# Attention weights copied into float32r tiles before they are transposed, in a one-core hybrid attention layer

## The chip, the core and the metric

The kernel runs on one NeuronCore of a Trainium2 chip. Its instructions go to five in-order queues: TensorE (PE; its weight loads are listed apart as PEld), VectorE (DVE), ScalarE (ACT), GpSimd (POOL) and SyncE (SP, which here only issues DMAs). The metric is the device time of one execution in microseconds, as the median of several runs. Operands are 4-byte floats. [...] 

## The reference

One residual layer over x (1024 x 1024). A conditioning vector gives a shift, a scale and a gate. The normalised input u is multiplied by a wide projection into queries, keys, values and gates of 16 heads of width 64. Eight heads are stick-breaking attention, eight are forgetting attention, both causal. The gated head outputs go through an output projection, and a residual and a layer norm end it:

```python
u = layer_norm(x) * (1 + scale) + shift
h = u @ w_in                        # q, k, v, g of 8 forgetting heads and of 8 stick-breaking heads
s = q @ k.T * 64 ** -0.5            # per head and block of 128 queries, keys up to the block's end
p = softmax(s + f_q - f_k)          # forgetting heads, masked causally
w = exp(log_sigmoid(s) + later)     # stick-breaking heads, later = sum of log_sigmoid(-s) of later keys
y = concat(p @ v, w @ v) * silu(g)
x = layer_norm(alpha * x + gate * (y @ w_out), ln_g, ln_b)
```

## The kernel before

**Units.** Heads go in eight pairs: 0 to 3 stick-breaking, 4 to 7 forgetting. A unit (p, h, i) is one head h of pair p and one block i of 128 queries against (i+1) x 128 keys, so there are 128 units, 16 per pair. A unit makes its scores on TensorE in PSUM (L483, L484), turns them into weights `be` or `a`, an SBUF tile of 128 queries by up to 1024 keys (ACT L506, L508, DVE scans L514, L518 and POOL L520, L521 for the stick-breaking pairs; DVE L491, ACT L496, POOL L499 for the others), and transposes them block by block on TensorE (L537), since the product with the values wants the keys on the partitions. Up to four transposes fill one PSUM tile `T`, of which there are two. ACT copies it out rounded (L539, hi) and DVE subtracts (L540, lo). The product with the values (`pv`, L554) runs for two query blocks at a time.

**Order on TensorE.** The order of TensorE is written out by hand. In turn k the scores of unit k are issued, and the transposes of unit k - LAG (LAG is 2), with `weights_turn`; `att_transpose` also puts waiting `pv` products behind its first T tile. Between them go "fillers", a generator of the projections of later pairs: `gen_m(p, m)` makes queries (m = 0), keys (1) or gates (2) of pair p in two PSUM accumulators, with 24 matmuls of 512 columns each, and `gen_v(g)` the values of two pairs in eight accumulators, with 24 matmuls of 256 columns each. The accumulators `acc` have two buffers. `FILL` says how many filler steps go into each pair's units. The other engines' orders come from a planner; a wait there holds up all that stands behind it on that engine.

**Tiles.** Queries and keys of a pair are four tiles of 128 x 1024 (one per head), from a ring `q` of four buffers and a ring `k` of four, so two pairs fit. `evac_k` fills half of a key tile by a DMA inside SBUF (L298). `xr`, the input block of the output stage, uses the same ring at the end.

Of the kernel before, what the change touches and what calls it, by code (L numbers as in the profile page):

```python
# [7 lines left out]

F32 = mybir.dt.float32
# [4 lines left out]
P = 128  # L14
# [3 lines left out]
NPAIR = 8  # L18
# [9 lines left out]
def tile_hybrid_layer(  # L28
# [30 lines left out]
    def pt_tile(name, dt=F32R, shape=None):  # L59
        return big("pt", 3, name, dt, shape or [P, 2, 1024])  # L60

    def acc_tile(name):
        return ps.tile([P, 512], F32, tag="acc", bufs=2, name=name)

# [23 lines left out]
        return stack  # L88


    ident = cp.tile([P, P], F32, tag="ident", name="ident")
    make_identity(nc, ident)
    causal = cp.tile([P, P], F32, tag="causal", name="causal")
    nc.gpsimd.memset(causal, 0.0)
    nc.gpsimd.affine_select(out=causal, in_=causal, pattern=[[-1, P]], base=0,
# [221 lines left out]
    key_casts = []  # L317

    def make_q(p):
        qst[p] = [big("q", 4, f"q_{p}_{h}", F32R) for h in range(2)]  # L320

    def make_k(p):
        kst[p] = [big("k", 4, f"k_{p}_{h}", F32R) for h in range(2)]
        klo[p] = big("kl", 2, f"kl_{p}", F32R)

    def make_g(p):
# [124 lines left out]
    def att_query(u):  # L451
# [3 lines left out]
        r = slice(h * HD, h * HD + HD)  # L455
        nc.scalar.copy(z[r, :], qst[p][h].bitcast(F32)[r, i * P:i * P + P])  # L456

    masks, scaled, lows, gates = [], [], [], []

    def att_causal(u):  # L460
# [9 lines left out]
    def att_scores(u, following):  # L470
        p, h, i = u
        z = zq.pop(u)
        ke = (i + 1) * P
        ns = 1 if ke <= 512 else 2
        w = ke // ns
        qs = slice(i * P, i * P + P)
        if p >= 4:
            f = fb[2 * (p - 4) + h]
        S = s_tile(f"S_{p}_{h}_{i}")
        halves = range(ns) if p >= 4 else range(ns)[::-1]  # L480
        for s in halves:
            ks = slice(s * w, s * w + w)
            nc.tensor.matmul(S[:, s, :w], qst[p][h][:, qs], kst[p][h][:, ks], start=True, stop=False)  # L483
            nc.tensor.matmul(S[:, s, :w], z, klo[p][:, ks], start=False, stop=True)  # L484
        v3 = lambda a: a[:, :ke].rearrange("p (a b) -> p a b", a=ns)
        if p >= 4:
            a = att_tile(f"a_{p}_{h}_{i}")
            nm = sb.tile([P, 1], F32, tag="nm", bufs=4, name=f"nm_{p}_{h}_{i}")
            l = sb.tile([P, 1], F32, tag="l", bufs=4, name=f"l_{p}_{h}_{i}")
            with after(*lows):  # L490
                nc.vector.tensor_tensor_reduce(out=v3(a), in0=S[:, :ns, :w], in1=v3(f),  # L491
                                               op0=ALU.add, op1=ALU.min, scale=-1.0, scalar=BIG,
                                               accum_out=nm)
            if following:
                att_causal(following)
            nc.scalar.activation(a[:, :ke], a[:, :ke], AF.Exp, scale=-1.0, bias=nm, accum_out=l)  # L496
            nc.vector.reciprocal(l, l)  # L497
            scaled[:] = [*scaled[-3:],
                         nc.gpsimd.tensor_scalar(a[:, :ke], a[:, :ke], l, 1.0, op0=ALU.mult, op1=ALU.mult)]  # L499
            st_w[u] = a  # L500
        else:
            kp = att_tile(f"kp_{p}_{h}_{i}")
            be = att_tile(f"be_{p}_{h}_{i}")
            with after(*key_casts):
                for s in halves:
                    nc.scalar.activation(kp[:, s * w:s * w + w], S[:, s, :w], AF.Sigmoid, scale=-1.0)  # L506
            key_casts.clear()
            last_act = nc.scalar.activation(v3(be), S[:, :ns, :w], AF.Sigmoid)  # L508
            gates[:] = [last_act]


            lo = ke - w
            rv = kp[:, lo:ke][:, ::-1]
            last_dve = nc.vector.tensor_tensor_scan(rv, rv, floor[:, :ke - lo], initial=0.0,  # L514
                                                    op0=ALU.mult, op1=ALU.max)
            if lo:
                rv = kp[:, :lo][:, ::-1]
                last_dve = nc.vector.tensor_tensor_scan(rv, rv, floor[:, P:P + 1].to_broadcast([P, lo]),  # L518
                                                        initial=kp[:, lo:lo + 1], op0=ALU.mult, op1=ALU.max)
            nc.gpsimd.tensor_tensor(be[:, :ke - 1], be[:, :ke - 1], kp[:, 1:ke], op=ALU.mult)  # L520
            nc.gpsimd.memset(be[:, ke - 1:ke], 0.0)  # L521
            st_w[u] = be
            return last_act, last_dve

    def att_transpose(u, between=()):
        p, h, i = u
        a = st_w.pop(u)
        j, qo = i // 2, (i % 2) * P
        for g in range((i // 4) + 1):
            n = min(4, i + 1 - 4 * g)  # L530
            if (p, h, j, g) not in st_pt:
                st_pt[p, h, j, g] = pt_tile(f"pt_{p}_{h}_{j}_{g}", F32R, [P, 2, 4, 256])
            hi, lo = (st_pt[p, h, j, g][:, x] for x in range(2))
            tp = t_tile(f"T_{p}_{h}_{i}_{g}")
            for b in range(n):
                kb = 4 * g + b
                nc.tensor.transpose(tp[:, b * P:(b + 1) * P], a[:, kb * P:(kb + 1) * P], ident)  # L537
            t3 = tp[:, :n * P].rearrange("p (a b) -> p a b", a=n)
            nc.scalar.copy(hi[:, :n, qo:qo + P], t3)  # L539
            lows[:] = [nc.vector.tensor_tensor(lo[:, :n, qo:qo + P], t3, hi.bitcast(F32)[:, :n, qo:qo + P],  # L540
                                               op=ALU.subtract)]
            while between:
                att_pv(*between.pop(0))
# [56 lines left out]

    def start_raw(n):
        if used[0] % 2 == 0:
            raws.append(big("qk"[len(raws) // 4], 4, f"raws_{len(raws)}"))
        a = used[0] % 2 * 512
        used[0] += n
        return raws[-1][:, a:a + n * 512]
# [336 lines left out]
    def o_half(t, h):  # L943
# [1 line left out]
        s = slice(*groups(t)[h])  # L945
        ng = len(groups(t))
        if h == 0:
            xr = big("k", 4, f"xr_{t}")
# [67 lines left out]
    def gen_last_g(p):  # L1016
# [26 lines left out]
    LEAD = 2  # L1043
    LAG = 2
    W0 = 100.0
    OUT0 = 4
    TAIL = (2, 2, 2, 2, 2, 2, 4, 4, 4, 4, 8)
# [35 lines left out]
    tail = chain([gen_out_first(6), gen_out_last(6)] + [gen_out(t) for t in OUT_ORDER[1:]])  # L1083
    fill(4)
    def weights_turn(k):
        if LAG <= k < len(units) + LAG:
            u = units[k - LAG]
            att_transpose(u, ready)
            seen.add(u)
            if (u[0], u[1], u[2] ^ 1) in seen:  # L1090
                ready.append((u[0], u[1], u[2] // 2))
        while k >= len(units) + LAG and ready:
            att_pv(*ready.pop(0))

    def scores_turn(k):
# [104 lines left out]
```

## Time and profile before

| | |
|---|---|
| runs, median of 3 | 680.42 us (680.38 to 680.78) |
| profiled execution, span from first to last instruction | 678.6 us |
| around the span (median less span) | 1.8 us |
| TensorE busy, granted clock | 668.3 us, 0.996 |
| transposes of weights on TensorE (L537) | 576 |
| DMA, all queues | 81.55 MB |

The page gives one profiled execution; "busy" sums instruction durations on an engine, and for TensorE, whose matmuls overlap, the distance between two starts tells more than a duration. The profiled execution's own time is taken as the median of the runs, 1.8 us above its span. Rows of a timeline read: start in us, us, engine, line, operation, output<-inputs, shape, count.

### The profile page before, as it was taken

How to read it: one execution, taken by the hardware profiler on the slowest of the kernel's cores; microseconds unless marked ns; L12 is line 12 of the kernel's file. 1: busy time of each engine (PE TensorE's matmuls, PEld its weight loads, DVE VectorE, ACT ScalarE, POOL GpSimd, SP SyncE). 2: the span in 40 equal slices, each digit the busy share in tenths (PEclk: the TensorE clock that was granted, in tenths of full speed). 3: DMA queues.
4: the chain of work that ended last, by engine and by line, in shares of the span. 5: the costliest groups of instructions: out<-in, count | busy, mean ns of one | idle time of the engine just before them, and what ended most of it. 6: DMA issues, size and time to landing. Idle time of an engine off the chain costs nothing.

```text
span 678.6 us, 11231 instructions
## 1 busy us (share of the span) xinstructions
PE 668.3 (98%) x3713; PEld 571.2 (84%) x3713; DVE 485.9 (72%) x1001; ACT 382.6 (56%) x889; POOL 405.2 (60%) x530
## 2 busy tenths in 40 slices
PE   8999999999999999999999999999999999999995
PEld 4888898888998888889988888889988888888885
DVE  6787779868677777686776675766676777775645
ACT  5576468757567667576675564655565766521000
POOL 5560279755357556556378878785785365655412
PEclk9999999999999999999999999999999999999998
DMA  9983432112101112122124555263452297153301
GB/s 326 401 312 126 139 79 75 41 28 67 29 20 56 54 42 57 40 54 56 49 93 144 151 164 174 87 201 112 127 169 59 70 350 302 59 177 107 120 32 63
DMA packets 46474, 81.55 MB, mean 120 GB/s; under 512 B 5264, under 2 KB 20176, under 8 KB 46416
## 3 DMA queue, kind: packets, MB, share of 16 engines
q1 hardware_dynamic: 44832, 76.37, 35.1%
q10 hardware_dynamic: 1584, 4.47, 2.1%
q8 instruction: 29, 0.48, 0.3%
q14 instruction: 29, 0.24, 0.1%
HBM read 60.34 MB, written 16.29 MB: 113 GB/s over the span
## 4 chain that ended last, share of the span: by engine, by line
PE 97%; DMA 1%; DVE 0%; POOL 0%; ACT 0%; issue 0%; SPq 0%; POOLq 0%
PE m L312 11%; PE m L314 10%; PE m L313 10%; PE pv L554 10%; PE T L537 9%; PE S L484 5%; PE S L483 5%; PE o L939 4%; PE o L937 4%; PE o L938 4%; PE v L370 4%; PE v L372 4%; PE v L371 4%; PE st_q L647 1%; PE st_k L647 1%; PE st_late L647 1%
## 5 line engine op out<-in xcount | busy, mean ns | idle before, releaser
L540 DVE TENSOR_TENSOR pt<-T,pt 128x512 fp32r<-128x512 f32 (+2 forms) x192 | 102.7, 553 | 43.8 <-ACT pt L539 42.2
L539 ACT CAST pt<-T 128x512 fp32r<-128x512 f32 (+2 forms) x192 | 88.9, 479 | 64.5 <-PE T L537 62.5
L312 PE MATMUL m<-uh,whi 128*128 128x512 f32 x304 | 123.3, 405 | 0.1
L314 PE MATMUL m<-uh,wlo 128*128 128x512 f32 x304 | 119.8, 394 | 0.0
L313 PE MATMUL m<-ul,whi 128*128 128x512 f32 x304 | 119.7, 394 | 0.0
L520 POOL TENSOR_TENSOR be<-be,kp 128x127 f32<-128x127 f32 (+3 forms) x64 | 78.9, 1234 | 36.2 <-DVE kp L518 24.4
L554 PE MATMUL pv<-pt,v 128*128 128x512 f32 x320 | 82.8, 388 | 0.0
L514 DVE TENSOR_TENSOR_SCAN kp<-kp,floor 128x128 f32<-128x128 f32 (+3 forms) x64 | 58.6, 915 | 17.6 <-ACT kp L506 17.4
L499 POOL TENSOR_SCALAR a<-a,l 128x1024 f32<-128x1024 f32 (+3 forms) x64 | 48.4, 756 | 34.3 <-DVE l L497 26.0
L483 PE MATMUL S<-k,q 128*128 128x512 f32 (+5 forms) x192 | 68.8, 360 | 0.0
L314 PEld LDWEIGHTS m<-uh,wlo 128*128 128x128 f32 x304 | 57.1, 188 | 13.7
L496 ACT ACTIVATE a<-a,nm 128x1024 f32<-128x1024 f32 (+3 forms) x64 | 49.8, 779 | 28.6 <-DVE nm L491 28.1
L312 PEld LDWEIGHTS m<-uh,whi 128*128 128x128 f32 x304 | 57.2, 188 | 10.2 <-PE T L537 0.3
L484 PE MATMUL S<-kl,qz 128*128 128x512 f32 (+5 forms) x192 | 65.2, 341 | 0.0
L313 PEld LDWEIGHTS m<-ul,whi 128*128 128x128 f32 x304 | 57.3, 188 | 9.0
L554 PEld LDWEIGHTS pv<-pt,v 128*128 128x128 f32 x320 | 55.5, 189 | 8.9
L570 POOL TENSOR_TENSOR ty<-ty,sg 64x256 f32<-64x256 f32 x64 | 46.9, 733 | 23.4 <-issue 12.2
L491 DVE CUSTOM_DVE_ANT_0 a<-S,fb 128x1024 f32<-128x1024 f32 (+3 forms) x64 | 48.2, 753 | 16.9 <-PE S L484 12.0
L456 ACT CAST qz<-q 64x128 fp32r<-64x128 f32 x128 | 37.3, 296 | 34.2 <-PE S L484 33.0
L506 ACT ACTIVATE kp<-S 128x384 f32<-128x384 f32 (+4 forms) x96 | 44.0, 494 | 21.5 <-PE S L484 20.2
L370 PE MATMUL v<-whi_v,uh 128*128 128x256 f32 (+1 forms) x192 | 54.7, 285 | 0.0
L372 PE MATMUL v<-wlo_v,uh 128*128 128x256 f32 (+1 forms) x192 | 54.2, 282 | 0.0
(296 smaller groups left out, 1628.3 us busy)
## 6 DMA issues: line engine op xcount, KB each, us to landing
raw<-in_w_qkg_dram SPq DMA_DIRECT2D x38, 256.0 KB, 2.7
wss<-in_w_ss_dram SPq DMA_DIRECT2D x14, 512.0 KB, 8.1
x<-in_x_dram SPq DMA_DIRECT2D x8, 512.0 KB, 7.1
k<-k SPq DMA_DIRECT2D x32, 128.0 KB, 2.3
wg<-in_w_gate_dram SPq DMA_DIRECT2D x8, 512.0 KB, 4.9
raw_o<-in_w_out_dram SPq DMA_DIRECT2D x16, 256.0 KB, 3.0
fb<-f_dr ACTq DMA_DIRECT2D x8, 512.0 KB, 4.5
wo_dr<-whi_o SPq DMA_DIRECT2D x16, 256.0 KB, 2.1
```

Source lines behind the costliest of these rows:

```text
L312: nc.tensor.matmul(acc, hi[:, c], u_hi[kt][:, s], start=(kt == 0), stop=False)
L313: nc.tensor.matmul(acc, hi[:, c], u_lo[kt][:, s], start=False, stop=False)
L314: nc.tensor.matmul(acc, lo[:, c], u_hi[kt][:, s], start=False, stop=(kt == NB - 1))
L370: nc.tensor.matmul(acc[:, :n], u_hi[kt][:, ts_], hi[:, s], start=(kt == 0), stop=False)
L372: nc.tensor.matmul(acc[:, :n], u_hi[kt][:, ts_], lo[:, s], start=False, stop=(kt == NB - 1))
L483: nc.tensor.matmul(S[:, s, :w], qst[p][h][:, qs], kst[p][h][:, ks], start=True, stop=False)
L484: nc.tensor.matmul(S[:, s, :w], z, klo[p][:, ks], start=False, stop=True)
L520: nc.gpsimd.tensor_tensor(be[:, :ke - 1], be[:, :ke - 1], kp[:, 1:ke], op=ALU.mult)
L537: nc.tensor.transpose(tp[:, b * P:(b + 1) * P], a[:, kb * P:(kb + 1) * P], ident)
L539: nc.scalar.copy(hi[:, :n, qo:qo + P], t3)
L540: lows[:] = [nc.vector.tensor_tensor(lo[:, :n, qo:qo + P], t3, hi.bitcast(F32)[:, :n, qo:qo + P], op=ALU.subtract)]
L554: nc.tensor.matmul(acc2[:, :, q0:], vt[p][:, kb, h * P:(h + 1) * P], pt[:, :, q0:], start=(kb == 0), stop=(kb == last))
```

## The change

The weights of pairs 1 to 6 are no longer transposed from the tile in which they were made. A new function `hop` copies them by a DMA on SP's queue, inside SBUF, into one of two float32r tiles, used in turn, and `att_transpose` transposes from there with a float32r identity and a float32r view of the PSUM tile. Pairs 0 and 7 stay as they were. 96 copies are added, of 128 rows by (i+1) x 512 bytes.

The two tiles are taken from queries' and keys'. The two rings are replaced by eight single tiles `qk0` to `qk7`. Tiles 4 and 5 are used by the copies, and from pair 2 on queries and keys rotate through the other six: the queries of pair n take the tiles of head 1 of pair n-2, its keys those of head 0 of pair n-1. `gen_v(1)`, `gen_v(2)` and `gen_v(3)` move ahead of the key projections of pairs 2, 4 and 6, with `FILL` adapted. `LAGS` replaces LAG: in pairs 1, 2, 3 and 6 a unit is transposed three turns after its scores, in the others two. The identity is built by the same two POOL instructions as before, now written as float32r and viewed as float32 elsewhere.

```diff
+    q_home, k_home = {0: (0, 1), 1: (2, 3)}, {0: (4, 5), 1: (6, 7)}
+    q_home[2], k_home[2] = (0, 1), (2, 6)
+    for n in range(3, NPAIR):
+        q_home[n] = q_home[n - 2][1], k_home[n - 2][1]
+        k_home[n] = q_home[n - 1][0], k_home[n - 1][0]
+    def slot_tile(n, name, dt=F32):
+        return big(f"qk{n}", 1, name, dt)
...
-    ident = cp.tile([P, P], F32, tag="ident", name="ident")
-    make_identity(nc, ident)
+    ident_r = cp.tile([P, P], F32R, tag="ident", name="ident")
+    ident = ident_r.bitcast(F32)
+    nc.gpsimd.memset(ident, 0.0)
+    nc.gpsimd.affine_select(out=ident_r, in_=ident, compare_op=ALU.not_equal, fill=1.0, base=0,
+                            pattern=[[-1, P]], channel_multiplier=1)
...
-        qst[p] = [big("q", 4, f"q_{p}_{h}", F32R) for h in range(2)]
+        qst[p] = [slot_tile(q_home[p][h], f"q_{p}_{h}", F32R) for h in range(2)]
-        kst[p] = [big("k", 4, f"k_{p}_{h}", F32R) for h in range(2)]
+        kst[p] = [slot_tile(k_home[p][h], f"k_{p}_{h}", F32R) for h in range(2)]
...
+    HOPS = range(1, 7)
+    hops = [0]
+    def hop(u, w, ke):
+        if u[0] not in HOPS:
+            return w
+        to = slot_tile((4, 5)[hops[0] % 2], f"w_{u[0]}_{u[1]}_{u[2]}", F32R)
+        hops[0] += 1
+        nc.sync.dma_start(to.bitcast(F32)[:, :ke], w[:, :ke])
+        return to
...
-            st_w[u] = a
+            st_w[u] = hop(u, a, ke)
-            st_w[u] = be
+            st_w[u] = hop(u, be, ke)
...
-                nc.tensor.transpose(tp[:, b * P:(b + 1) * P], a[:, kb * P:(kb + 1) * P], ident)
+                if p in HOPS:
+                    nc.tensor.transpose(tp.bitcast(F32R)[:, b * P:(b + 1) * P], a[:, kb * P:(kb + 1) * P], ident_r)
+                else:
+                    nc.tensor.transpose(tp[:, b * P:(b + 1) * P], a[:, kb * P:(kb + 1) * P], ident)
...
-        gen_m(2, 0), gen_m(2, 1), gen_v(1),
+        gen_m(2, 0), gen_v(1), gen_m(2, 1),
-        gen_m(4, 0), gen_m(4, 1), gen_v(2),
+        gen_m(4, 0), gen_v(2), gen_m(4, 1),
-                      gen_m(6, 0), gen_m(6, 1), gen_v(3), gen_m(6, 2),
+                      gen_m(6, 0), gen_v(3), gen_m(6, 1), gen_m(6, 2),
-    FILL = (52, 72, 68, 68, 72, 72, 58, 16)
+    FILL = (52, 76, 68, 72, 68, 74, 52, 16)
+    LAGS = (2, 3, 3, 3, 2, 2, 3, 2)
...
-        if LAG <= k < len(units) + LAG:
-            u = units[k - LAG]
+        for n in (3, 2):
+            if not 0 <= k - n < len(units) or LAGS[units[k - n][0]] != n:
+                continue
+            u = units[k - n]
             att_transpose(u, ready)
```

The order moves at three places that matter here. In names such as `T_3_1_7_0` the numbers are pair, head, block and T tile, and the last one counts buffers; `m_4_2_1` is the gate projection of pair 4, second half; `S` are scores.

The first place is TensorE at the turn from pair 3 to pair 4, where three turns of lag become two. Before, the transposes of unit (3,1,7) are followed by projections:

```order
L537 MATMUL T_3_1_7_0_4160<-ident_66,be_3_1_7_4022 128x128 [waits DVE_49,Pool_49]
L537 MATMUL T_3_1_7_0_4160<-ident_66,be_3_1_7_4022 128x128 x3
L537 MATMUL T_3_1_7_1_4167<-ident_66,be_3_1_7_4022 128x128 [waits DVE_49]
L537 MATMUL T_3_1_7_1_4167<-ident_66,be_3_1_7_4022 128x128 x3
L312 MATMUL m_4_2_1_4099<-uh_6_130,whi_4_2_1_4071 128x512
L313 MATMUL m_4_2_1_4099<-ul_6_138,whi_4_2_1_4071 128x512
L314 MATMUL m_4_2_1_4099<-uh_6_130,wlo_4_2_1_4072 128x512
```

and those of unit (4,0,7) come with 19 rows between. With the change both units stand in one turn:

```order
L564 MATMUL T_3_1_7_0_4332<-ident_66,w_3_1_7_4167 128x128 [waits DMAHW6_49,DVE_49]
L564 MATMUL T_3_1_7_0_4332<-ident_66,w_3_1_7_4167 128x128 x3
L564 MATMUL T_3_1_7_1_4339<-ident_66,w_3_1_7_4167 128x128 [waits DVE_49]
L564 MATMUL T_3_1_7_1_4339<-ident_66,w_3_1_7_4167 128x128 x3
L564 MATMUL T_4_0_7_0_4347<-ident_66,w_4_0_7_4204 128x128 [waits DMAHW1_49,DVE_49]
L564 MATMUL T_4_0_7_0_4347<-ident_66,w_4_0_7_4204 128x128 x3
L583 MATMUL pv_3_1_3_4354<-pt_3_1_3_0_4265,v_3_1763 128x512 [waits Activation_49]
L583 MATMUL pv_3_1_3_4354<-pt_3_1_3_0_4265,v_3_1763 128x512 x3
```

Three T tiles follow each other, and the transposes wait for a DMA where they waited for POOL. The same turn stands between pairs 6 and 7, for units (6,1,0) and (7,0,7).

The second place is ACT in pair 1, where the value accumulators `v_1_t` are emptied (`v_2` and `v_3` are the value tiles of pairs 2 and 3). Before, this falls into the first units of head 1:

```order
L378 CAST v_2_1955<-v_1_3_2142 128x2x64
L539 CAST pt_1_1_0_0_2111<-T_1_1_1_0_2172 128x2x128
L506 ACTIVATE kp_1_1_3_2180<-S_1_1_3_2177 128x512
L378 CAST v_3_1956<-v_1_3_2142 128x2x64
L508 ACTIVATE be_1_1_3_2181<-S_1_1_3_2177 128x512
L456 CAST qz11_83<-q_1_1_262 64x128
L378 CAST v_2_1955<-v_1_4_2188 128x2x64
L378 CAST v_3_1956<-v_1_4_2188 128x2x64
```

With the change it falls into the last units of head 0, whose rows are longer:

```order
L568 CAST pt_1_0_2_1_1995<-T_1_0_4_1_1996 128x128
L532 ACTIVATE kp_1_0_7_2005<-S_1_0_7_2000 128x512 x2
L534 ACTIVATE be_1_0_7_2006<-S_1_0_7_2000 128x1024
L596 COPY ty_1_0_1_2016<-pv_1_0_1_1990 64x256
L470 CAST qz01_81<-q_2_0_1564 64x128
L392 CAST v_2_1762<-v_1_4_1963 128x2x64
L568 CAST pt_1_0_2_0_1982<-T_1_0_5_0_2053 128x4x128
L392 CAST v_3_1763<-v_1_4_1963 128x2x64
```

The casts of `v_1_4` now stand behind the three sigmoids of unit (1,0,7).

The third place is SP's queue, also in pair 1, after the change: the copies (L481) stand between the loads of raw projection weights (L137) and the stores of head outputs (L607).

```order
L481 DMA w_1_0_0_1608<-be_1_0_0_1602 128x128 [waits PE_49,Activation_49,Pool_49]
L607 DMA y_dr_91<-ty_0_1_2_1610 64x256 [waits DMAHW6_49,Pool_49]
L481 DMA w_1_0_1_1660<-be_1_0_1_1654 128x256 [waits PE_49,Activation_49,Pool_49]
L137 DMA raw_2_1_1_2217<-in_w_qkg_dram 128x512 [waits DMAHW2_49,DMAHW0_49,Pool_49]
L481 DMA w_1_0_2_1686<-be_1_0_2_1680 128x384 [waits DMAHW1_49,PE_49,DMAHW5_49,Activation_49,Pool_49]
```

A copy waits for POOL's result (the weights) and for TensorE (the transposes of two units before, which read the same tile), and what stands behind it on SP waits with it.

More of the change, by code (lines that the diff above doesn't have):

```diff
@@ L5 @@
 from concourse import mybir
-from concourse.masks import make_identity
 from concourse._compat import with_exitstack
@@ L602, in start_raw @@
         if used[0] % 2 == 0:
-            raws.append(big("qk"[len(raws) // 4], 4, f"raws_{len(raws)}"))
+            raws.append(slot_tile(len(raws), f"raws_{len(raws)}"))
         a = used[0] % 2 * 512
@@ L947, in o_half @@
         if h == 0:
-            xr = big("k", 4, f"xr_{t}")
+            n = OUT_ORDER.index(t) % 4
+            xr = slot_tile((q_home[NPAIR - 2][1], k_home[NPAIR - 2][1], *k_home[NPAIR - 1])[n], f"xr_{t}")
             nc.sync.dma_start(xr, x[ts_, :])
@@ L1091, in weights_turn @@
                 ready.append((u[0], u[1], u[2] // 2))
-        while k >= len(units) + LAG and ready:
+        while k >= len(units) + LAGS[NPAIR - 1] and ready:
             att_pv(*ready.pop(0))
```

## The prediction

> **What bounds the kernel now.** I read the engines' shares, then the chain that ended last, then TensorE's waits.
>
> ```profile
> PE 668.3 (98%) x3713; PEld 571.2 (84%) x3713; DVE 485.9 (72%) x1001; ACT 382.6 (56%) x889; POOL 405.2 (60%) x530
> ...
> PE 97%; DMA 1%; DVE 0%; POOL 0%; ACT 0%; issue 0%; SPq 0%; POOLq 0%
> PE m L312 11%; PE m L314 10%; PE m L313 10%; PE pv L554 10%; PE T L537 9%; PE S L484 5%; PE S L483 5%; PE o L939 4%; PE o L937 4%; PE o L938 4%; PE v L370 4%; PE v L372 4%; PE v L371 4%; PE st_q L647 1%; PE st_k L647 1%; PE st_late L647 1%
> ```
> ```profile
> PE sc_all L179 <- POOL ident masks.py:199: 1.5, 1, 1.5
> PE xT_early L256 <- ACT x L222: 0.9, 1, 0.9
> PE st_q L647 <- ACT uh L270: 0.4, 1, 0.4
> ```
>
> TensorE is the chain, 97% of it, and waited 2.8 us in all, at the start. So time taken out of TensorE's stream is gained in full until another wait appears, and a new wait costs in full as well. The weights' transposes (T L537) are 9% of the chain.
>
> **What a transpose costs now, and what limits it.** First the matmuls, then the weight loads (PEld), around one unit's six transposes:
>
> ```profile
> L537 PE MATMUL T<-ident,be x288: 270/272/331, 86.3 to 351.5; 128*128 128x128 f32 x144
> ```
> ```profile
> 302.99 0.40 PE L314 MATMUL m<-uh,wlo 128*128 128x512 f32 x1
> 303.23 0.82 PE L537 MATMUL T<-ident,be 128*128 128x128 f32 x6
> 303.81 0.48 PE L483 MATMUL S<-k,q 128*128 128x512 f32 x1
> 304.12 0.40 PE L484 MATMUL S<-kl,qz 128*128 128x512 f32 x1
> ```
> ```profile
> 303.78 0.19 PEld L483 LDWEIGHTS S<-k,q 128*128 128x128 f32 x1
> 303.89 0.19 PEld L484 LDWEIGHTS S<-kl,qz 128*128 128x128 f32 x1
> ```
>
> Six transposes span 0.82 us and one lasts 0.27, so starts are (0.82 - 0.27) / 5 = 0.110 us apart. Behind the sixth (start 303.78) the scores' weights need their own load, 303.78 to 303.89, before the scores run. A transpose is a load of the attention weights and a pass of the identity. Either could set the 0.110. These rows tell them apart:
>
> ```profile
> 8.61 0.14 PEld L256 LDWEIGHTS xT_early<-ident,x 128*128 128x128 f32 x1 [0.33 <-ACT x L222]
> 8.67 0.14 PEld L256 LDWEIGHTS st_k<-ident,x 128*128 128x128 f32 x1
> ```
> ```profile
> L483 PE MATMUL S<-k,q x192: 221/362/505, 79.6 to 605.7; 128*128 128x384 f32 x48, 128*128 128x512 f32 x48, 128*128 128x320 f32 x32, 128*128 128x448 f32 x32
> ```
> ```profile
> 92.34 0.22 PE L483 MATMUL S<-k,q 128*128 128x128 f32 x1
> 92.40 0.27 PE L484 MATMUL S<-kl,qz 128*128 128x128 f32 x1
> ...
> 92.68 0.28 PE L371 MATMUL v<-whi_v_3b,ul 128*128 128x256 f32 x1
> 92.80 0.28 PE L372 MATMUL v<-wlo_v_3b,uh 128*128 128x256 f32 x1
> ```
> ```profile
> 92.34 0.19 PEld L484 LDWEIGHTS S<-kl,qz 128*128 128x128 f32 x1
> 92.45 0.19 PEld L370 LDWEIGHTS v<-whi_v_3b,uh 128*128 128x128 f32 x1
> ```
>
> After an idle stretch two transposes' loads start 0.06 us apart (8.61, 8.67): the load alone takes 0.06, so the pass sets the 0.110. A float32r matmul of the same 128 columns starts its successor after 0.06 (92.34, 92.40), and the shortest of them lasts 221 ns against 272 for a transpose, 51 ns less: a float32r pass over 128 columns is half as long. Against that, plain float32r loads follow each other at no less than 0.11 (92.34, 92.45), twice a transpose's load.
>
> So a float32r transpose costs at best max(0.06 load, 0.06 pass) = 0.06, and at worst 0.11, if its load is as long as other float32r loads. A load's length here goes with being a transpose: in the early rows float32 transposes load in 0.14 where every other load in these rows takes 0.19. I take 0.058 (estimate, both rows unrounded being about that).
>
> [...]
>
> **The gain.** Pairs 1 to 6 have 6 x 72 = 432 of the 576 transposes. The last of each uninterrupted run gains nothing, because the next product's load takes 0.11 behind it anyway. In the new order the 432 stand in 119 runs, so 432 - 119 = 313 gain 0.110 - 0.058 = 0.052 us: **16.0 us** (rounding 0.051). Bounds 0 and 16.
>
> **What it adds.** The durations:
>
> ```profile
> L539 ACT CAST pt<-T 128x512 fp32r<-128x512 f32 x96 | 55.4, 586 | 24.7 <-PE T L537 23.5
> L378 ACT CAST v<-v 128x128 fp32r<-128x128 f32 x60 | 16.0, 267 | 19.4 <-DVE v L379 9.8 <-PE v L372 8.9
> L506 ACT ACTIVATE kp<-S 128x512 f32<-128x512 f32 x24 | 13.6, 604 | 1.2 <-PE S L484 0.8
> L508 ACT ACTIVATE be<-S 128x1024 f32<-128x1024 f32 x8 | 8.3, 1042 | 0.0
> ```
> ```profile
> L540 DVE TENSOR_TENSOR pt<-T,pt 128x512 fp32r<-128x512 f32 x96 | 65.2, 686 | 26.4 <-ACT pt L539 25.7
> L514 DVE TENSOR_TENSOR_SCAN kp<-kp,floor 128x512 f32<-128x512 f32 x16 | 19.4, 1214 | 1.5 <-ACT kp L506 1.3
> L379 DVE TENSOR_TENSOR v<-v,v 128x128 fp32r<-128x128 f32 x60 | 17.0, 285 | 8.8 <-ACT v L378 8.0
> ```
>
> *Value projections beside long units.* A value accumulator takes 24 x 0.12 = 2.9 us of TensorE, and with two buffers must be emptied within that. Emptying is four dependent steps, ACT, DVE, ACT, DVE: 2 x (0.27 + 0.29) = 1.1 us. Behind a unit of eight blocks, as the order on ACT now has it, the first step waits for 2 x 0.60 + 1.04 = 2.2 us of sigmoids, and DVE may be in two scans of 1.2. That is 1.1 + 2.2 = 3.3 us, 0.4 over the cover, up to 5.7 with the scans, 2.8 over. Three value projections moved, each meeting one such unit or its forgetting counterpart: 3 x (0.4 to 2.8), or nothing where the cover holds. I take the lower middle, 1.3 each: **3.9 us**.
>
> *Two units in one turn*, between pairs 3 and 4 and between 6 and 7. The third T tile reuses the first, which must be copied and subtracted: 0.59 + 0.69 = 1.28 us, against some 0.25 of transposes between. 1.0 of TensorE waits, up to 2.2 more if sigmoids stand ahead; I take 1.4. At the second place the `pv` of unit (6,1,0) follows its own transpose with four others (0.44) between, and needs both steps on one block; I take 0.6. Together **2.0 us**, bounds 0 and 5.
>
> *The copies.* The nearest rows are a copy inside SBUF of 128 KB and a load of 512 KB:
>
> ```profile
> k<-k SPq DMA_DIRECT2D x32, 128.0 KB, 2.3
> ...
> xr<-in_x_dram SPq DMA_DIRECT2D x8, 512.0 KB, 3.5
> ```
> ```profile
> q1 hardware_dynamic: 44832, 76.37, 35.1%
> ```
>
> A copy of up to 512 KB takes some 2 to 3.5 us, 4 behind another. It needs to fit between POOL's last step and the transposes. Two tight units of before, the first in a pair that now has a turn more, the second in pair 5, which has not:
>
> ```profile
> 242.85 2.00 POOL L520 TENSOR_TENSOR be<-be,kp 128x1023 f32<-128x1023 f32 x1 [1.52 <-DVE kp L518]
> ```
> ```profile
> 245.31 0.93 PE L537 MATMUL T<-ident,be 128*128 128x128 f32 x7
> ```
> ```profile
> 422.88 1.12 POOL L499 TENSOR_SCALAR a<-a,l 128x1024 f32<-128x1024 f32 x1
> ```
> ```profile
> 426.63 0.60 PE L537 MATMUL T<-ident,a 128*128 128x128 f32 x4
> ```
>
> The first had 245.31 - 244.85 = 0.46 us left; one more turn, 4.1 us by the first quoted row of transposes (86.3 to 351.5 for the 64 units of four pairs), leaves 4.6 for 3.5. The second had 426.63 - 424.00 = 2.6 for 3.5: **0.9 us** short. Other units of pairs 4 and 5 I take as covered; bounds 0 and, were four units so short, 3.6.
>
> *At nothing:* the identity, two POOL instructions as before. The bytes: 96 copies of 64 KB times 4.5 blocks on average are 27.6 MB on 76.4, which takes the queue's share of the DMA engines from 35% to some 48%. SP's issuing: behind a copy that waits for POOL stand raw weight loads, for whose users TensorE has rounded weights in a ring of five, and stores that are read in the output stage alone. Fewer tiles for keys and queries, since the new order puts each key projection's end behind head 0's last scores of the pair before. If that cover is gone, TensorE waits for keys at a pair's first scores, at most one DMA of 2.3 us per pair.
>
> **The sum.** 680.4 - 16.0 + 3.9 + 2.0 + 0.9 = **671.2 us** (in the profile's terms a span of 678.6 - 9.2 = 669.4).
>
> **The rivals.**
>
> *The load binds, slower.* The 432 transposes keep 0.11 because their loads, now float32r, take 0.11. For it: every float32r load in the trace; against it: the short loads of the transposes. Nothing is won and the waits stay: 680.4 + 6.8 = 687.2, from 680.4 to 695. It decides as soon as the load is over 0.088 us (16.0 x (0.110 - load) / 0.052 = 6.8). A float32r transpose that passes twice, so that the change doesn't do what it says, gives the same.
>
> *The copies are late as a rule.* In pairs 4 and 5 (32 units, two turns) SP holds copies behind POOL's results of other work. At 0.9 us for a third of them, 10 us more: 681. For it: the one order on SP; against it: POOL's 60% load, and no wait of TensorE on POOL before.
>
> *No new wait at all.* The stalls find cover, as before, where TensorE waited for nothing behind the start: 664.4. The same planner's orders had no stall before, but three T tiles in a row and the casts behind three sigmoids speak against it.
>
> **How the numbers follow.** Forecast 0.70, within it 664.4 to 679 by the bounds above (costs 0 to 15); load binds 0.18; copies late 0.07; no wait 0.05. The range 664 to 684 leaves out most of the load's case (about 0.12) and a little below. Within 0.2% (1.4 us), about what a measurement here can tell from no change, lie parts of the forecast's upper end and of the late copies: 0.05. Faster 0.73, slower 0.22.
>
> **What would show it.** Right: groups of six float32r transposes of some 0.56 us (5 x 0.058 + 0.27 or less) in place of 0.82, a pass of about 0.22, loads of 0.14, and T's busy share down. Waits of TensorE for DVE at the value accumulators of pairs 1, 3 and 5 and at the turn from pair 3 to 4, near 1.3 us each. Wrong: transposes still 0.11 apart, with loads of 0.19, or TensorE's waits for DMA among the longest.

## The result and the profile after

The changed kernel takes **690.36 us** (median of 4 runs, 690.24 to 691.28) against 680.40 in the runs of before beside it: a ratio of 1.0149, 95% interval 1.0135 to 1.0163, so about 10 us slower. I forecast 671.2, and the range ended at 684. The profiled span is 688.6 us against 678.6. Of all executions below, one (725.42 us at a mean granted clock of 0.849, in the run with three turns in pairs 4 and 5 too) lies far above the others of its kernel and is left out.

First the engines' shares and the chain that ended last, of the changed kernel:

```profile
PE 667.2 (97%) x3713; PEld 565.9 (82%) x3713; DVE 484.8 (70%) x1001; ACT 381.6 (55%) x889; POOL 406.1 (59%) x530
...
PE 84%; DMA 5%; DVE 4%; ACT 2%; issue 2%; POOL 2%; SPq 1%; POOLq 0%; DVEq 0%; ACTq 0%
```

TensorE was 97% of the chain before and is 84% now; DMA and DVE have entered it. How much TensorE stands still is read from two long stretches, first of the kernel before, then of the changed one (us, then busy us of each engine, granted clock, DMA share, GB/s):

```profile
100.00:350.00 250.00, 249.98 (x1475) 218.95 (x1474) 190.61 (x326) 170.17 (x403) 153.50 (x205) 1.00 0.20 51
350.00:570.00 220.00, 219.95 (x1224) 188.92 (x1223) 152.04 (x395) 130.37 (x315) 157.15 (x179) 1.00 0.50 159
```
```profile
100.00:350.00 250.00, 246.17 (x1460) 214.13 (x1459) 185.25 (x316) 165.21 (x394) 156.48 (x207) 1.00 0.34 108
350.00:570.00 220.00, 211.89 (x1180) 179.48 (x1179) 147.60 (x385) 126.37 (x308) 147.56 (x169) 0.98 0.61 204
```

TensorE idled 0.1 us in these 470 us before and idles (250 - 246.17) + (220 - 211.89) = 11.9 us now, two thirds of it in the second stretch, where the DMA engines' share goes from 0.50 to 0.61 and the mean clock is 0.98. What ended its waits:

```profile
PE T L564 <- DVE pt L569: 4.2, 4, 1.9
PE T L564 <- DMA w<-a: 2.9, 3, 1.8
PE v L384 <- DVE q L300: 1.6, 1, 1.6
...
PE v L384 <- DVE v L393: 1.1, 1, 1.1
PE pv L583 <- DVE pt L569: 0.8, 2, 0.6
PE v L384 <- DVE fsb L396: 0.8, 1, 0.8
```

The four longest stalls behind the start, in the timeline (the wait stands in brackets):

```profile
213.90 0.54 PE L564 MATMUL T<-ident,w 128*128 128x128 f32 x4 [1.70 <-DVE pt L569]
...
362.66 0.61 PE L564 MATMUL T<-ident,w 128*128 128x128 f32 x4 [1.86 <-DVE pt L569]
...
442.67 0.39 PE L384 MATMUL v<-whi_v,uh 128*128 128x256 f32 x1 [1.61 <-DVE q L300]
...
563.15 0.28 PE L564 MATMUL T<-ident,w 128*128 128x128 f32 x1 [1.85 <-DMA w<-a]
```

And what became of the transposes (the matmuls and weight loads of L564: shortest, median, longest in ns):

```profile
L564 PEld LDWEIGHTS T<-ident,w x432: 137/140/223, 146.8 to 563.1; 128*128 128x128 f32 x144
L564 PE MATMUL T<-ident,w x432: 220/245/317, 147.0 to 563.1; 128*128 128x128 f32 x144
```

The pass did halve: the first two of the six at 312.16 start 0.06 us apart (they span 0.28 and one lasts 0.22) where 0.11 stood before, and the shortest is 220 ns as forecast, where 270 stood. But a group of six now spans 0.62 to 0.63 us where 0.56 was forecast. So three questions for the experiments: what the float32r transposes are worth, what the copies cost, and what the new order costs without either.

### The profile page after: what moved, and what is told of

It is laid out like the page before. It is cut to its first block, busy times and chain, and to the rows that moved or that the text cites. A ratio compares the mean times of both kernels' runs of the same rounds, so it can differ in the third digit from the quotient of the medians.

```text
span 688.6 us, 11586 instructions
## 1 busy us (share of the span) xinstructions
PE 667.2 (97%) x3713; PEld 565.9 (82%) x3713; DVE 484.8 (70%) x1001; ACT 381.6 (55%) x889; POOL 406.1 (59%) x530
## 4 chain that ended last, share of the span: by engine, by line
PE 84%; DMA 5%; DVE 4%; ACT 2%; issue 2%; POOL 2%; SPq 1%; POOLq 0%; DVEq 0%; ACTq 0%
PE pv L583 10%; PE m L326 8%; PE m L327 8%; PE m L328 8%; PE S L509 4%; PE o L968 4%; PE o L966 4%; PE o L967 4%; PE S L510 4%; PE T L564 4%; PE v L384 4%; PE v L386 4%; PE v L385 4%; DMA w<-a 3%; PE T L566 2%
## 5 line engine op out<-in xcount | busy, mean ns | idle before, releaser
L564 PEld LDWEIGHTS T<-ident,w 128*128 128x128 f32 x432 | 47.6, 141 | 19.1 <-DVE pt L569 6.2
L564 PE MATMUL T<-ident,w 128*128 128x128 f32 x432 | 52.0, 238 | 7.2 <-DVE pt L569 4.2
```

The lines of the kernel that those rows point to most:

```text
L564: nc.tensor.transpose(tp.bitcast(F32R)[:, b * P:(b + 1) * P], a[:, kb * P:(kb + 1) * P], ident_r)
```

## The experiments

All medians are set against runs of the kernel before on the same chip (680.1 to 680.5). A difference between two kernels here is uncertain by some 1 to 2 us. Edits are shown in part where a line with three dots stands in them.

### What the transposes are worth

**Float32r without copies.** The kernel before, with its order of TensorE's work; the engine that computes the weights writes them rounded, as float32r:

```diff
-            a = att_tile(f"a_{p}_{h}_{i}")
+            a = att_tile(f"a_{p}_{h}_{i}", F32R if 1 <= p <= 6 else F32)
-            be = att_tile(f"be_{p}_{h}_{i}")
+            be = att_tile(f"be_{p}_{h}_{i}", F32R if 1 <= p <= 6 else F32)
...
+                if 1 <= p <= 6:
+                    nc.tensor.transpose(tp.bitcast(F32R)[:, b * P:(b + 1) * P], a[:, kb * P:(kb + 1) * P], ident_r)
...
```

> The kernel before, its order of TensorE's work kept and a lag of two for every pair, but the weights of pairs 1 to 6 are written as float32r by the engine that computes them, so that they are transposed as float32r without a copy. What is left out: the part of each weight (and of each forgetting head's sigmoids) that float32r does not hold, so the output is a little coarser. Theory (the float32r transposes follow each other at 0.081 us instead of 0.110, and the product behind a run starts 0.057 instead of 0.029 us behind it, so 0.028 us on 432 - 2 x 119 transposes): 5.4 us faster, about 675. Rival A, the prediction's own term (0.052 us on 313): 664.4. Rival B, the product behind each run gives all of it back: 680.4.

Measured: 674.66 us (673.82 to 675.06), ratio 0.9917 [0.9902, 0.9931], 5.6 us faster. The theory's 675 holds; the prediction's own term (664.4) is 10 us off, and "no gain" is out as well.

**Why 5.6 and not 16: the load.** The same six transposes in this kernel, the matmuls and then the weight loads:

```profile
300.81 0.63 PE L541 MATMUL T<-ident,be 128*128 128x128 f32 x6
301.27 0.47 PE L486 MATMUL S<-k,q 128*128 128x512 f32 x1
```
```profile
300.81 0.48 PEld L541 LDWEIGHTS T<-ident,be 128*128 128x128 f32 x5
301.24 0.19 PEld L486 LDWEIGHTS S<-k,q 128*128 128x128 f32 x1
```

Five loads of 0.14 span 0.48, so they start (0.48 - 0.14) / 4 = 0.085 us apart, and the last passes follow them. Before, five spanned 0.57:

```profile
303.23 0.57 PEld L537 LDWEIGHTS T<-ident,be 128*128 128x128 f32 x5
```

that is (0.57 - 0.14) / 4 = 0.108, set by the float32 pass. So the pass no longer binds, and the load does, at 0.085: not the 0.06 that I had read from two loads after an idle stretch. From the first transpose to the next product is 301.27 - 300.81 = 0.46 us against 303.81 - 303.23 = 0.58, so six transposes gain 0.12 us, which is 5 x (0.110 - 0.085) and not 5 x 0.052 = 0.26.

With 0.085 the prediction's own formula gives 313 x 0.025 = 7.8 us, and the whole trace bears that out. I summed the distances between starts over the transposes of pairs 1 to 6, before and here. Inside the runs they fall from 33.9 to 22.2 us. From a run's last transpose to the product behind it they rise from 3.7 to 9.7 (medians of 120 runs: 28 and 84 ns; one wait of 0.67 us not counted). From that product to the matmul after it they fall from 35.5 to 33.6. In all 7.6 us are gained. Inside a run the starts lie closer (0.071 on average) than the loads do, and the end of the run pays for it, so the prediction's rule for the ends holds only in sum. The kernel gains 5.6 and not 7.6, as TensorE has two waits that the kernel before doesn't have:

```profile
PE v L375 <- POOL wlo_v L131: 0.8, 1, 0.8
PE m L315 <- DVE kl L302: 0.7, 1, 0.7
```

By the distance between starts a wait takes some 0.17 us more than its bracket says, since the matmul before it is booked with its whole length (0.28 us for 256 columns, 0.40 for 512, where starts lie 0.12 and 0.23 apart); these two take some 1.8 us.

**Is the short load that of a transpose?** The same kernel, with ordinary products in the transposes' place:

```diff
-                    nc.tensor.transpose(tp.bitcast(F32R)[:, b * P:(b + 1) * P], a[:, kb * P:(kb + 1) * P], ident_r)
+                    nc.tensor.matmul(tp[:, b * P:(b + 1) * P], lhsT=a[:, kb * P:(kb + 1) * P], rhs=ident_r, start=True, stop=True)
```

> As the kernel that rounds the weights of pairs 1 to 6 where they are written, but each of these transposes is an ordinary float32r product of the weights with the identity. What is left out: as there, the part of the weights that float32r does not hold. Theory (a short load goes with a transpose, an ordinary load of 128 columns takes 0.11, which then sets the distance): 432 - 120 distances of 0.110 in place of 0.081, so 674.7 + 9 = 683.7. Rival (the load's length does not go with the transpose, 0.081 is the distance of float32r passes): 674.7.

Measured: 681.08 us (680.71 to 681.32), ratio 1.0010 [1.0001, 1.0020].

```profile
L541 PEld LDWEIGHTS T<-ident,be x216: 187/190/193, 143.9 to 351.7; 128*128 128x128 f32 x108
```
```profile
303.43 0.64 PEld L541 LDWEIGHTS T<-ident,be 128*128 128x128 f32 x5
```

The load of the same data is 190 ns long instead of 140, and loads start (0.64 - 0.19) / 4 = 0.113 us apart. So the load's length goes with the transpose, as I had argued, and an ordinary product of 128 columns would have won nothing. The time rose by 6.4 us where 9 were expected. By the same sum of distances the ordinary products take 8.4 us more, and the two waits of the kernel above (1.8 us) are gone in this one.

**All eight pairs.**

```diff
-                if 1 <= p <= 6:
+                if 0 <= p:
...
```

> As the kernel that rounds the weights where they are written, for all eight pairs. What is left out: the part of every weight that float32r does not hold. Pairs 0 and 7 have 144 more transposes in 40 more runs. Theory (0.028 us on 144 - 2 x 40): 674.7 - 1.8 = 672.9. Rival (in pairs 0 and 7, whose units are short, the product behind gives it back): 674.7 or above.

Measured: 673.72 us (673.26 to 674.54), ratio 0.9903 [0.9888, 0.9918]; the step from 674.7 is 0.9 where 1.8 was expected, no more than this measurement can tell. This is the lowest median here, ahead of both kernels, at the price that the expectation names: the remainders of the weights are lost.

**The transposes' gain inside the changed kernel.** The copied tile, transposed as float32:

```diff
-                    nc.tensor.transpose(tp.bitcast(F32R)[:, b * P:(b + 1) * P], a[:, kb * P:(kb + 1) * P], ident_r)
+                    nc.tensor.transpose(tp[:, b * P:(b + 1) * P], a.bitcast(F32)[:, kb * P:(kb + 1) * P], ident)
```

> The changed kernel, with copies, lags and order, but the copied tile is read as float32 and transposed as before. This takes away the float32r transposes alone. Theory (they are worth 5.4 us where they stand): 690.4 + 5.4 = 695.8, less what of the longer transposes covers the new waits, so 693 to 696. Rival A (they are worth 16.0, as predicted, and the new waits cost 26): 706. Rival B (they are worth nothing): 690.4.

Measured: 694.34 us (692.61 to 696.15), ratio 1.0208 [1.0185, 1.0231]. The float32r transposes are worth 4.0 us where they stand, in the expected 693 to 696; the 16 of the prediction would have shown as 706. By the sum of distances they gain 6.9 us here. Part of it is lost again at the value accumulators. With float32 transposes TensorE waits there for 0.15, 0.20 and 0.38 us, in the changed kernel, at the same three places, for 0.76, 1.12 and 1.61:

```profile
PE v L384 <- DVE q L300: 0.4, 1, 0.4
...
PE v L384 <- DVE v L393: 0.2, 1, 0.2
PE v L384 <- DVE fsb L396: 0.2, 1, 0.2
```

So most of the value stalls comes with the faster transposes. I read it so that TensorE reaches the accumulator sooner, and ACT and DVE are no sooner done with it.

### What the copies cost

**No copies.**

```diff
-    HOPS = range(1, 7)
+    HOPS = ()
```

This makes the transposes float32 again as well, so the run is set against the one above.

> The changed kernel with its tiles, lags and order of filling work, without the copies: the weights are transposed as float32 from where they were computed. Theory (new waits by order and lag some 10 us, copies the other 4 to 5 us): 680.4 + 10 = 690 to 691. Rival A (the copies cause nearly all the new waits, through late landings and SP's queue): 680 to 682. Rival B (the copies cost nothing, order and lag everything): 695.

Measured: 689.22 us (688.24 to 690.26), ratio 1.0131 [1.0114, 1.0148]. So tiles, lags and order alone cost 8.8 to 9.1 us, and copies that are read cost 694.3 - 689.2 = 5.1 more.

**Copies that nobody waits for.**

```diff
-    HOPS = range(1, 7)
+    HOPS = ()
...
-        if u[0] not in HOPS:
+        if u[0] not in range(1, 7):
             return w
...
         nc.sync.dma_start(to.bitcast(F32)[:, :ke], w[:, :ke])
-        return to
+        return w
```

> The changed kernel with all its copies issued, but each unit transposed as float32 from where it was computed, so no transpose waits for a copy; a copy's tile is free as soon as the copy before it has landed. Theory (the copies' 5.1 us come from transposes that wait for a landing): 689.2 to 690, as without copies. Rival (they come from SP's queue and the DMA traffic): 693 to 694, as with copies that are read.

Measured: 687.83 us (687.71 to 688.26), ratio 1.0111 [1.0096, 1.0126]; as without copies, even 1.4 us less, which is no more than this measurement can tell. SP's issuing and the bytes as such cost TensorE nothing that shows. The price is paid where a transpose waits for its copy: three waits of 3.9 us together in the kernel that reads its copies as float32, none here. In the changed kernel such waits are 2.9 us, and one of them is 1.85:

```profile
554.85 0.48 SPq L481 DMA_DIRECT2D w<-a  x1
```
```profile
q1 hardware_dynamic: 1406, 3.92, 89.1%
...
w<-a SPq DMA_DIRECT2D x1, 64.0 KB, 8.3
```
```profile
DMA to landing us min/median/max: 1.8/2.7/8.3
```

Unit (6,1,0) has the smallest copy of all, 64 KB, and the longest landing: issued at 554.85, it landed 8.3 us later, at 563.15, when its transpose ran. Between 552 and 564 us (the second fence) SP's queue keeps the DMA engines at 89%, with the loads of the output weights. A median of 2.7 us is what the prediction reckoned with; most of the wait came from this one copy, in the stretch where the engines were full. The wait takes in more than the landing: POOL had the weights of this unit ready at 551.64, 3.2 us before the copy was issued.

SP itself held the copies longer for another reason than for POOL (44.0 us in all). By the view of its own waits:

```profile
SPq L481 <- PE T L564: 115.5, 54, 4.5
```

With two tiles, a copy must wait until TensorE has transposed the unit two before. That wait, 115.5 us in 54 copies and up to 4.5 in one, has no term in the prediction's sum. The copies that nobody reads have no such wait, so no run here separates how much of the 5.1 is a late issue and how much a slow landing.

**Copies in pairs 1 to 3 alone.**

```diff
-    HOPS = range(1, 7)
+    HOPS = range(1, 4)
```

> The changed kernel with copies and float32r transposes in pairs 1 to 3 alone, pairs 4 to 6 transposed as float32 from where they were computed. Theory (the late landings all lie in pairs 4 to 6, so the copies of pairs 1 to 3 cost nothing, and 216 transposes in 60 runs gain 0.028 x (216 - 120) = 2.7): 689.2 - 2.7 = 686.5. Rival (the copies cost as much in each pair): 689.2 + 2.6 - 2.7 = 689.1.

Measured: 688.18 us (687.54 to 690.23), ratio 1.0121 [1.0101, 1.0141], between the theory's 686.5 and the rival's 689.1: the time does not tell them apart. The trace does in part. No transpose waits for a copy in it, so the late copies do lie in pairs 4 to 6. And the value stalls of pairs 1 and 3, which have float32r transposes here, are 0.76 and 1.12 us as in the changed kernel, while that of pair 5, which has not, is 0.69 instead of 1.61.

### What tiles, lags and order cost

**The tiles alone.** No copies, `LAGS` all 2, `FILL` and the projections as before:

```diff
-    HOPS = range(1, 7)
+    HOPS = ()
...
-        gen_m(2, 0), gen_v(1), gen_m(2, 1),
+        gen_m(2, 0), gen_m(2, 1), gen_v(1),
...
-    FILL = (52, 76, 68, 72, 68, 74, 52, 16)
+    FILL = (52, 72, 68, 68, 72, 72, 58, 16)
...
-    LAGS = (2, 3, 3, 3, 2, 2, 3, 2)
+    LAGS = (2, 2, 2, 2, 2, 2, 2, 2)
```

> Of the changed kernel only the fewer tiles for keys and queries: no copies, weights transposed as float32, a lag of two, the projections in the order and the shares of before. Theory (the tiles cost nothing, as predicted; the late keys of the kernel without copies and with a lag of two came from the value projections' place): 680.4, no gap over 0.25 us. Rival (a key projection now has to wait until the pair before has read its queries, so its accumulators hold TensorE): 684 to 688, with waits of TensorE for keys or key accumulators.

Measured: 684.62 us (683.48 to 684.87), ratio 1.0059 [1.0044, 1.0074], 4.2 us slower. The theory (nothing) falls. The one stall of this trace behind the start, and ACT in front of it:

```profile
169.95 0.39 PE L384 MATMUL v<-whi_v,uh 128*128 128x264 f32 x1 [2.55 <-DVE kl L313]
```
```profile
167.26 1.06 ACT L308 CAST k<-m 64x512 fp32r<-64x512 f32 x2
168.22 0.30 ACT L470 CAST qz<-q 64x128 fp32r<-64x128 f32 x1
168.59 1.18 ACT L308 CAST k<-m 64x512 fp32r<-64x512 f32 x2
```

The keys of pair 2 go to tiles that head 0 of pair 1 still used; its last scores start at 167.01 on TensorE. In ACT's order all four key casts of pair 2 stand behind that, DVE's four subtractions behind them, and the values' accumulators wait for both. In the kernel before, with a ring of four, DVE had done two of these four at 159.8 and 161.1. The prediction put the tiles at nothing "since the new order puts each key projection's end behind head 0's last scores", and this run has the old order. With the new order, in the kernel without copies and in the changed kernel, no wait of TensorE for keys or for a key's subtraction is left: the cover that the prediction counted on holds there.

**Tiles and lags.** Against the kernel with the tiles alone:

```diff
-    LAGS = (2, 2, 2, 2, 2, 2, 2, 2)
+    LAGS = (2, 3, 3, 3, 2, 2, 3, 2)
```

> As the kernel with the fewer tiles alone, and the changed kernel's lags (three turns in pairs 1, 2, 3 and 6). Theory (the gaps that the kernel without copies shows at the table loads, 1.8, at the turn from pair 3 to 4, 1.8, in pair 6, 1.0, and at the turn from pair 6 to 7, 0.6 + 1.6 + 0.5, are the lag's): 680.4 + 7.3 = 687.7. Rival A (the places of the value projections make them): 680.4 to 682. Rival B (with a lag of three and the shares of before the keys come late as well): 692 or more.

Measured: 690.9 us (690.03 to 691.59), ratio 1.0154 [1.0139, 1.0169], so the lags cost 6.3 us over the tiles. That is near the theory's 7.3, but by luck: of the gaps that it named, none stands at the table loads, and those at the turns and in pair 6 are 1.05, 0.72 + 0.53 + 0.25 and 0.27, 2.8 in all.

```profile
PE v L384 <- DVE kl L313: 4.1, 2, 2.5
PE T L566 <- DVE pt L569: 1.6, 3, 1.1
```

Another 1.59 is a second stall behind the key casts, at 313.86, that the tiles alone did not have, and at the end of the first the granted clock is 0.50 for 3.4 us, which takes up to 1.7. The changed kernel without copies has the value projections moved on top, at 689.2: that gives back 1.7, as the key stalls (4.1) go and others come.

One of these others is at the table loads. ACT in the changed kernel, ahead of the stall at 213.90:

```profile
209.59 1.28 ACT L422 ACT_TABLE_LOAD   x1
210.88 0.26 ACT L422 ACTIVATE fab<-fab 128x64 f32<-128x64 f32 x1
211.15 1.28 ACT L424 ACT_TABLE_LOAD   x1
212.44 0.21 ACT L424 ACTIVATE cm<-c_sb 128x8 f32<-128x8 f32 x1
212.56 0.84 ACT L568 CAST pt<-T 128x512 fp32r<-128x512 f32 x2
```

The forgetting heads' preparation loads two tables, 1.28 us each. The kernel before has the same two, from 210.3 to 213.2, and no stall: there the next unit's transposes came while they ran, with T tiles free. In the changed kernel the T tiles are full when the tables are loaded, the casts that empty them stand behind 3.0 us of ACT, and TensorE waits 1.7. The lag alone does not do it: with tiles and lags, but the projections where they were, the casts come at 210.50, ahead of the tables at 212.21, and there is no stall; nor is there one in the next run, with the projections moved and a lag of two. It takes both.

**The lag of two, with the value projections moved.**

```diff
-    HOPS = range(1, 7)
+    HOPS = ()
...
-    FILL = (52, 76, 68, 72, 68, 74, 52, 16)
+    FILL = (52, 72, 68, 68, 72, 72, 58, 16)
...
-    LAGS = (2, 3, 3, 3, 2, 2, 3, 2)
+    LAGS = (2, 2, 2, 2, 2, 2, 2, 2)
```

> The changed kernel's tiles and order of projections, without copies (weights transposed as float32) and with a lag of two for all pairs and the shares of filling work by pair as before. Theory (the lag makes most of the 9.1 us by which the kernel without copies is slower than before; the value projections' places make 0.3 + 0.3 + 0.9): 680.4 + 1.5 = 681.9, with no gap where two units met in a turn or at the forgetting heads' table loads. Rival (the places of the projections and the fewer tiles for keys and queries make it): 687 to 689.

Measured: 692.39 us (690.66 to 694.48), ratio 1.0177 [1.0156, 1.0199], the opposite of the 681.9 expected. The stalls of the lag are gone, as said, but two others come, at the first scores of pairs 4 and 6:

```profile
PE S L509 <- DMA k<-k: 6.9, 2, 3.9
```

With `gen_v` ahead of the keys and the shares of before, the keys are made too late for the next pair. So the run does not isolate the lag: `FILL` and the projections' places hang together, and I had taken them for two things.

**Three turns in pairs 4 and 5 too.**

```diff
-    LAGS = (2, 3, 3, 3, 2, 2, 3, 2)
+    LAGS = (2, 3, 3, 3, 3, 3, 3, 2)
```

> The changed kernel with pairs 4 and 5 transposed three turns behind their scores as well, so that only the turn from pair 6 to 7 has two units, and copies of pairs 4 and 5 have a turn more. Theory (the three gaps at the turn from pair 3 to 4, 2.0 + 0.3 + 0.4 us, and the late copies of pairs 4 and 5, 1.0 + 0.4, are due to that lag): 690.4 - 4.1 = 686.3, and no gap at the turn from pair 3 to 4. Rival (the lag of three itself is what holds ACT's and DVE's steps up, by putting transposes behind other work than before): pairs 4 and 5 get stalls of their own, 690 or more.

Measured: 684.65 to 688.33 us in three executions, ratio 1.0087 [1.0062, 1.0113], so 1.0087 x 680.4 = 686.3 us, as the theory has it. The stall at 362.66 is gone: the eight transposes at 360.17 run through. That much is shown. But the two small gaps that the theory named beside it stay (0.29 us at 348.30, 0.35 at 355.36), and a copy is still late by 1.12 at 507.85, so the match of the sum is in part luck. The longest wait left is the late copy, now 2.28 us, at the turn from pair 6 to 7:

```profile
557.74 0.28 PE L564 MATMUL T<-ident,w 128*128 128x128 f32 x1 [2.28 <-DMA w<-a]
```

**Value projections behind the keys.**

```diff
-        gen_m(2, 0), gen_v(1), gen_m(2, 1),
-        beside(chain([gen_m(2, 2), gen_m(3, 0), gen_m(3, 1), gen_m(3, 2)]), gen_forget()),
+        gen_m(2, 0), gen_m(2, 2), gen_m(2, 1), gen_v(1),
+        beside(chain([gen_m(3, 0), gen_m(3, 1), gen_m(3, 2)]), gen_forget()),
...
```

> The changed kernel with its copies, but the value projections of pairs 1, 3 and 5 put behind the key projections of the next pair, as they stood before, and the gate projections put where they stood. Theory (the three stalls of TensorE at value accumulators, 0.93 + 1.28 + 1.78 us in the changed kernel's trace, come from that place): 690.4 - 4.0 = 686.4, all three gone from the trace. Rival (they come from ACT's and DVE's queues being fuller everywhere, and meet whatever stands there): 690.4, with waits of the same length at the same time for other accumulators.

Measured: 688.38 us (686.27 to 690.07), ratio 1.0118 [1.0097, 1.0140], half of the 4.0 us expected (the expectation counts the stalls by the distance between starts, 0.17 more each). The three stalls are gone from their places, and one of 2.2 stands at another:

```profile
348.82 0.36 PE L384 MATMUL v<-whi_v,uh 128*128 128x256 f32 x1 [2.23 <-DVE v L393]
```

Now the values of pairs 4 and 5 meet the long units at the end of pair 3. So the place of the values decides where TensorE stalls. That it stalls at all goes, by the runs above, with the faster transposes.

## Why the prediction was wrong

The runs give the change as a ladder (medians, us; each step uncertain by 1 to 2, and worth what it says in this order of steps alone):

| step | run | from before | predicted |
|---|---|---|---|
| fewer tiles for keys and queries | 684.6 | +4.2 | 0 |
| lags of three | 690.9 | +6.3 | +2.0 |
| value projections ahead, `FILL` | 689.2 | -1.7 | +3.9 |
| copies, read as float32 | 694.3 | +5.1 | +0.9 |
| transposes in float32r | 690.4 | -4.0 | -16.0 |
| sum | | +10 | -9.2 |

- **The gain, 16.0 us: the step that failed.** It is 12 of the 19 us by which I missed. The mechanism was right (the pass halves, 0.06 us against 0.11; a transpose's load is shorter than another's, 140 ns against 190), the size was not: "the load alone takes 0.06" came from two loads behind an idle stretch, and in a stream they start 0.085 apart. With that the formula gives 7.8, and 7.6 were measured by distances. The prediction named 0.088 as the point from which the change is not worth its waits and 0.11 as the only other bound. It had no row of a stream of transposes limited by loads, since the float32 passes, 0.11 apart, hid the loads' distance, and it took the lower end; the value lay in the middle of the two. Of the 6.9 us that the transposes gain in the changed kernel, the time shows 4.0: TensorE, come sooner, waits longer at the values.
- **Values, 3.9.** The three stalls came as forecast, at pairs 1, 3 and 5: 0.8, 1.1 and 1.6 us against 1.3 each, but not by the place alone. With float32 transposes at the same place they are 0.7 together. In the ladder they stand mostly in the last row, not in the third.
- **Tiles at nothing.** In the changed kernel no wait for keys is left, so this held. The 4.2 of the first row belongs to the old order of the projections; the first and third rows together are 2.5.
- **Two units in one turn, 2.0.** The stall at the turn from pair 3 to 4 is 1.86 where 1.4 was taken, so this was near. What the lags cost beyond it has no term in the sum: the changed order puts transposes against work that I had not looked at, like the table loads (1.70).
- **The copies, 0.9.** The two late copies in pairs 4 and 5 (0.82 and 0.20 us) are what was taken, and the median landing (2.7) fits the 2 to 3.5 reckoned. The third, 1.85, is in pair 6, which the prediction took as covered by its extra turn. What I left out is that a mean share of 48% (45% came) says nothing of the stretch at 89%, where 64 KB took 8.3 us, and that a copy waits for its tile. "TensorE's waits for DMA among the longest" was named as a sign that the forecast is wrong, and they are second.
- **The clock.** Two stretches of half clock behind waits take 3.3 us in the profiled execution; the prediction has no such term. The last section is on this.
- **The rivals.** "The load binds" was the nearest: its 687.2 with nothing won is closer than my 671.2. But the transposes won 4.0, and everything else cost 14 us instead of 6.8.

## What to carry to other kernels

Two loads that started after an idle stretch did not give the distance of a stream (0.06 us against 0.085): look for a row in which the resource that is to bind next already binds, and where there is none, do not take the best end of the bounds. Time won on the bounding engine also brought it sooner to tiles that others had to empty, so part of it came back as waits (of 6.9 us won, the time kept 4.0). In this kernel, whose TensorE had waited 0.1 us in 470, the freedoms that the edit takes (a tile, a turn, two units in one turn) were paid in stalls, and several small ones added up to more than the gain. A rounding that is asked of the engine that writes the tile anyway (5.6 us faster) costs no copy, though it gives up the weights' remainders; a copy in a stretch where the DMA queue is full (89% here, a landing of 8.3 us against a median of 2.7) has to be priced there, not by its median.

## What the runs showed of the hardware

**A stall cost twice here.** Windows of the changed kernel (columns as above): the wait at the turn from pair 3 to 4, the time behind it, and the time behind the late copy:

```profile
361.00:362.60 1.60, 0.00 (x0) 0.00 (x0) 1.60 (x5) 1.49 (x4) 1.42 (x3) 1.00 0.09 20
362.60:366.20 3.60, 3.54 (x12) 2.87 (x13) 1.56 (x5) 0.59 (x1) 1.66 (x2) 0.55 0.91 312
563.10:566.00 2.90, 2.63 (x12) 2.20 (x13) 1.45 (x4) 1.33 (x4) 0.97 (x1) 0.72 1.09 380
566.00:569.00 3.00, 3.00 (x12) 2.44 (x11) 1.08 (x2) 0.47 (x1) 2.38 (x4) 0.71 1.02 411
```

Behind a wait of 1.86 us the granted clock is 0.55 for 3.6 us, which takes 3.6 x 0.45 = 1.6 us of full speed, and behind the other 2.9 x 0.28 + 3.0 x 0.29 = 1.7. In the kernel with late keys, after a wait of 3.9, products of 512 columns start 0.43 us apart (495.45 and 495.88) where they start 0.23 apart elsewhere:

```profile
494.46 0.77 PE L509 MATMUL S<-k,q 128*128 128x512 f32 x1 [3.86 <-DMA k<-k]
495.03 0.63 PE L510 MATMUL S<-kl,qz 128*128 128x512 f32 x1
495.45 0.63 PE L326 MATMUL m<-uh,whi 128*128 128x512 f32 x1
495.88 0.63 PE L327 MATMUL m<-ul,whi 128*128 128x512 f32 x1
```

So some 3.3 us of the changed kernel's profiled execution can be clock, not wait. Whether the other executions lose as much is open: their mean clocks, which also count the time behind the last product, go with the time in some kernels (with the tiles alone 683.48 us at 0.997, 684.61 to 684.87 at 0.994 and 0.995), but not in the changed one (690.29 us at 0.992, 690.24 at 0.996). Over all traces here, behind the first 100 us, ten waits of TensorE were 1.85 to 3.86 us long, and nine of them had a stretch of half clock at their end or within 1.6 us of it; the tenth, 2.55 us in the kernel with the tiles alone, had none. Of seventeen waits of 1.27 to 1.72 us one had it. So in these traces length goes with it, but not length alone. The slow stretches are 3.4 us long each; in the kernel with late keys two stand behind each other after the wait of 3.86.

**Transposes loaded faster than products.** In these runs the same 128 x 128 float32r data loads in 140 ns and every 0.085 us as a transpose, in 190 ns and every 0.113 us as an ordinary product.
